# The down projection of a two-layer encoder by Strassen's scheme: seven products in place of eight, on one Trainium2 core

## The chip, the cores and the metric

The kernel runs on one core of one Trainium2 chip. The metric is the device time of one execution in microseconds (us), from the first to the last of the core's work; the time of before is the median of three runs.

## The reference

Two layers of a bidirectional encoder over 256 tokens of width 1024, float32. Each layer has a mixer (gated convolution, pooling and windowed attention) and then a gated feed-forward, which is where the change lies:

```python
    h2 = rms_norm(x, g_ffn)
    gate, up = jnp.split(h2 @ w_gu, [D_FF], axis=-1)     # D_FF = 2816
    return x + (jax.nn.silu(gate) * up) @ w_down         # w_down: 2816 x 1024
```

After the second layer one more RMSNorm gives the output.

## The kernel before, in words

Activations are held transposed: 128 rows of the model width on the partitions, the 256 tokens along the free axis. Each weight matrix is cut into 128 x 128 blocks. `plan_layer` (L36) lists the blocks of a layer in the order of use, and the host lays the stream out in that order, 16 blocks (1 MB) to a chunk. SyncE loads chunks into three buffers. A half-chunk of 8 blocks is one job of `convert` (L128): ScalarE rounds it to `hi` in the matmul's reduced format (L135), VectorE takes the rest, `lo = raw - hi` (L136). There are five `hi` and five `lo` buffers, so that a convert can start once the half-chunk five jobs earlier has been used. `advance` (L139), called when a half-chunk is first used, issues the next loads and converts.

Each product is three matmuls, for float32 accuracy: `hi` of the weights with `hi` and with `lo` of the activations, and `lo` of the weights with `hi` (`mm3`, L160 to L164). There the weights are stationary and 256 tokens move. The function `split` (L232) makes `hi` and `lo` of an activation on ScalarE and VectorE.

`ffn` (L590) works in 11 steps `q`. A step computes two gate tiles and two up tiles (32 blocks of `w_gu`, each tile the sum of 8 blocks), then the activation: sigmoid on ScalarE, times the gate, times up (L634 to L651). Its two result tiles are two of the 22 row blocks of `w_down`. The down products of step `q - 1` follow the gate and up tiles of step `q`. They are added up in four PSUM banks (`acc`), which stay occupied for the whole feed-forward; the gate and up tiles rotate through the four other banks (`newB`).

- In step 0 and 1 the input `xg` is not yet normalised: the tokens' factor `r` arrives late (`norm_stats`, `norm_rows`), and the activation applies it (L638, L641). From step 2 on the normalised tiles `hs` are used, which `make_h` (L304) computes on VectorE and ScalarE during step 0's activation.
- In layer 0 the down product has the weights stationary and 256 tokens moving (`down`, L597). The result is transposed like `x`, and `add_x` (L587) adds it bank by bank; the last two row blocks are taken bank by bank, so that the first bank ends first. `xg_tiles` (L241) and `squares` then make layer 1's inputs.
- In layer 1 the activations are stationary and 512 columns of `w_down` move (`down_nat`, L608 to L617); the result has tokens on the partitions. The four token and column quarters of `x` are transposed on TensorE during steps 4 to 7 (L671 to L676), and at the end `sums` (L718) adds a bank to each, squares it, and `rstd` and `store` write the output.

The instructions are written in the order of the source, and the framework's scheduler orders each engine's queue when the program is built: an instruction that is not ready by its estimate lets a later one pass. On the chip the queues of VectorE and ScalarE run in that order. The framework also keeps two engines from using one PSUM bank at a time.

## Time and profile before

| | us |
|---|---|
| median of 3 runs | 981.78 (981.57 to 982.46) |
| the profiled execution, its span | 980.1 |
| TensorE busy | 968.1 |
| VectorE busy | 715.7 |
| ScalarE busy | 554.0 |
| GpSimd busy | 45.7 |

The rows in the prediction name an engine (PE is TensorE's matmuls, PEld its weight loads, DVE VectorE, ACT ScalarE, POOL GpSimd), a line of the kernel, an operation with `output<-inputs`, the shape, and the count. In a list by time the first two numbers are the start and the duration; in brackets stands the idle time before it and what ended it. Matmuls are pipelined: their recorded durations overlap, and the pace is the distance between starts.

### The profile page before, as it was taken

The page shows a single profiled execution, that of the slowest core. Times are in us where ns is not written, and L with a number is a line of the kernel's source. Part 1 is how long each engine was busy: PE and PEld are TensorE (multiplying, and loading weights), DVE is VectorE, ACT ScalarE, POOL GpSimd, SP SyncE. Part 2 cuts the span into 40 slices and gives each one's busy share as a digit, 9 for nine tenths or more (in the row PEclk, how much of TensorE's full clock was granted, in tenths as well). Part 3 has the DMA queues.
Part 4 walks back from the last instruction along what each step waited for, and adds up shares of the span by engine and source line. Part 5 has one row for each costly group of instructions (what it writes and reads, how often), then busy time and mean ns, then how long its engine had stood idle before and what let it go on. Part 6 is the DMA issues. An engine that isn't in the chain of part 4 may idle for free.

```text
span 980.1 us, 19200 instructions
## 1 busy us (share of the span) xinstructions
PE 968.1 (99%) x7877; PEld 954.4 (97%) x7877; DVE 715.7 (73%) x1332; ACT 554.0 (57%) x931; POOL 45.7 (5%) x66
## 2 busy tenths in 40 slices
PE   8999999999999999999999999999999999999996
PEld 7999999999999999999999999999999999999995
DVE  7899898567668955545589898985777697555554
ACT  5866776654456544444477576765554564444443
POOL 5100000000001000000020000000000020000001
PEclk9999999999999999999999999999999999999999
DMA  8755544555554455455443745445554555545531
GB/s 279 254 193 197 189 161 163 197 180 183 189 199 171 174 189 199 173 178 205 178 172 130 248 163 188 161 143 174 192 193 173 172 194 189 200 170 204 184 129 43
DMA packets 27112, 178.12 MB, mean 182 GB/s; under 512 B 3280, under 2 KB 3808, under 8 KB 6800
## 3 DMA queue, kind: packets, MB, share of 16 engines
q1 hardware_dynamic: 24912, 169.93, 49.1%
q0 software_dynamic: 2112, 6.97, 2.5%
q8 instruction: 61, 1.00, 0.4%
q14 instruction: 27, 0.22, 0.1%
HBM read 175.80 MB, written 1.08 MB: 180 GB/s over the span
## 4 chain that ended last, share of the span: by engine, by line
PE 97%; DMA 1%; DVE 1%; SPq 0%; ACT 0%; issue 0%; DVEq 0%; ACTq 0%
PE b L162 25%; PE b L164 25%; PE b L163 25%; PE dn L164 2%; PE dn L162 2%; PE dn L163 2%; PE dn L617 2%; PE dn L616 2%; PE dn L615 2%; PE wo L162 2%; PE wo L163 2%; PE o L389 2%; PE wo L164 2%; PE pt L374 1%; DMA x<-xT 1%; PE sc L348 1%
## 5 line engine op out<-in xcount | busy, mean ns | idle before, releaser
L136 DVE TENSOR_TENSOR lo<-raw,hi 128x1024 fp32r<-128x1024 f32 (+1 forms) x321 | 390.0, 1222 | 215.2 <-ACT hi L135 214.4
L135 ACT ACTIVATE hi<-raw 128x1024 fp32r<-128x1024 f32 (+1 forms) x321 | 337.2, 1055 | 333.1 <-PE b L163 215.0
L162 PE MATMUL b<-h,hi 128*128 128x256 f32 x1344 | 379.8, 283 | 0.0
L164 PE MATMUL b<-h,lo 128*128 128x256 f32 x1344 | 378.4, 282 | 0.0
L163 PE MATMUL b<-h,hi 128*128 128x256 f32 x1344 | 378.3, 281 | 0.0
L162 PEld LDWEIGHTS b<-h,hi 128*128 128x128 f32 x1344 | 253.2, 188 | 0.2
L163 PEld LDWEIGHTS b<-h,hi 128*128 128x128 f32 x1344 | 253.1, 188 | 0.2
L164 PEld LDWEIGHTS b<-h,lo 128*128 128x128 f32 x1344 | 253.1, 188 | 0.0
L163 PE MATMUL b<-xg,hi 128*128 128x256 f32 x448 | 126.6, 283 | 1.6 <-DVE xg L250 1.6
L162 PE MATMUL b<-xg,hi 128*128 128x256 f32 x448 | 126.3, 283 | 1.1 <-DVE xg L247 0.8
L164 PE MATMUL b<-xg,lo 128*128 128x256 f32 x448 | 126.0, 282 | 0.0
L163 PEld LDWEIGHTS b<-xg,hi 128*128 128x128 f32 x448 | 84.4, 188 | 2.3 <-DVE xg L250 2.2
L162 PEld LDWEIGHTS b<-xg,hi 128*128 128x128 f32 x448 | 84.2, 188 | 1.6 <-issue 1.1
L164 PEld LDWEIGHTS b<-xg,lo 128*128 128x128 f32 x448 | 84.4, 188 | 0.0
L164 PE MATMUL dn<-fa,lo 128*128 128x256 f32 x176 | 49.5, 281 | 0.0
L163 PE MATMUL dn<-fa,hi 128*128 128x256 f32 x176 | 49.5, 281 | 0.0
L162 PE MATMUL dn<-fa,hi 128*128 128x256 f32 x176 | 49.5, 281 | 0.0
L260 POOL TENSOR_TENSOR sq<-sq,sq 128x512 f32<-128x512 f32 x12 | 16.2, 1353 | 507.3 <-DVE xg L250 315.5
L358 ACT ACTIVATE s<-s,sm 128x256 f32<-128x256 f32 x64 | 31.8, 500 | 13.0 <-DVE sm L355 13.0
L162 PE MATMUL b<-z,hi 128*128 128x256 f32 x128 | 36.4, 284 | 0.0
L164 PE MATMUL b<-z,lo 128*128 128x256 f32 x128 | 36.1, 282 | 0.0
L164 PE MATMUL b<-ao,lo 128*128 128x256 f32 x128 | 36.0, 282 | 0.0
(174 smaller groups left out, 1537.9 us busy)
## 6 DMA issues: line engine op xcount, KB each, us to landing
raw<-wst SPq DMA_DIRECT2D x158, 1024.0 KB, 4.9
bias<-stab POOLq DMA_DIRECT2D x16, 384.0 KB, 3.9
raw<-wst SPq DMA_DIRECT2D x3, 512.0 KB, 7.7
out<-xn SPq DMA_DIRECT2D x4, 256.0 KB, 2.0
x<-xT SPq DMA_DIRECT2D x3, 256.0 KB, 8.2
raw<-wst SPq DMA_DIRECT2D x2, 256.0 KB, 4.2
gf<-gfin POOLq DMA_DIRECT2D x2, 256.0 KB, 3.8
x<-xT SPq DMA_DIRECT2D x2, 128.0 KB, 4.6
```

The lines of the kernel that those rows point to most:

```text
L135: S.activation(hi[:, s], raw[:, s], AF.Copy)
L136: V.tensor_tensor(lo[:, s], raw[:, s], hi[:, s].bitcast(F32), op=ALU.subtract)
L162: PE.matmul(dst, wh, xh, start=start, stop=False, skip_group_check=skip)
L163: PE.matmul(dst, wh, xl, start=False, stop=False, skip_group_check=skip)
L164: last_mm[0] = PE.matmul(dst, wl, xh, start=False, stop=stop, skip_group_check=skip)
L260: G.tensor_tensor(st["acc"], st["acc"], sq, op=ALU.add)
L348: PE.matmul(ps[:, half(j)], qs[t][j][:, cs], kh, start=True, stop=False)
L358: S.activation(s[:, j], s[:, j], AF.Exp, bias=sm[:, 2 + j:3 + j], accum_out=sm[:, 6 + j:7 + j])
L389: PE.matmul(ps[:, half(j)], vv, pts[kt][i][:, half(j)], start=(kt == i == 0), stop=(kt == i == 1))
L615: PE.matmul(d, ah[:, cs], wh, start=(k == 0), stop=False)
L616: PE.matmul(d, ah[:, cs], wl, start=False, stop=False)
L617: PE.matmul(d, al[:, cs], wh, start=False, stop=(k == FT - 1))
```

## The change

A step's share of the down projection is a product of 2 x 2 blocks: token halves (128 tokens) by row blocks (the step's two), times row blocks by column halves (512 columns). Strassen's scheme in Winograd's form has seven block products where the plain one has eight, with sums of blocks on both sides and on the results.

- **Activations** (`forms`): the four blocks F and four sums of them, F2 (four VectorE operations on 128 columns), all split into `hi` and `lo`. They are the stationary operands; 512 weight columns move.
- **Weights** (`convert`, `take_forms`): a step's `w_down` rows are one chunk. Its jobs are A (two blocks, 1024 columns), B (one block, 512), C and D (two sums each, 1024). VectorE makes the sums in float32 from the raw chunk, right behind B's conversion.
- **Results**: seven PSUM banks hold the seven running sums M1 to M7 over all 11 steps. One bank (`G_`) is left for the gate and up tiles from step 2 on: the gate tile in its first half, the up tile in its second. So the gate, up pair of one tile is computed, then the down products of A and B of the step before, then the next pair, then C and D.
- **Activation function**: Silu on ScalarE in place of sigmoid and a multiplication on VectorE.
- **End of a layer**: the last two steps' products stand together; then VectorE combines the banks (`u2`, `u3`, `v` and the four quarters). In layer 0 the quarters, tokens on the partitions, are transposed back on TensorE (16 transposes) for `add_x`. In layer 1 the transposed `x` (and a difference of two parts of it) is put into four of the banks before the first products, so that the sums include it; the separate transposes and the additions of `x` at the end are gone.

The core of the diff:

```diff
     for q in range(NQ):
...
         else:
-            inner("gu", ns)
-        if q >= 1:
-            for k in (2 * q - 2, 2 * q - 1):
-                out.extend(("down", k, m) for m in range(8))
...
+            inner("gu", ns[0::2])
+            if q < NQ - 1:
+                down(first, q - 1)
+            inner("gu", ns[1::2])
+            if q < NQ - 1:
+                down(second, q - 1)
+    down(first + second, NQ - 2)
+    down(first + second, NQ - 1)
...
+    def convert(i):
+        c, f, _ = JOBS[i]
+        raw = raws[c]
+        n = HT * P // 2 if f == "B" else HT * P
+        if f in ("A", "B"):
+            src = raw[:, 0:n] if f == "A" else raw[:, 3 * n:4 * n]
+        elif f in ("C", "D"):
+            src = sums_[c][f == "D"]
...
+        if f == "B":
...
+            V.tensor_tensor(t.rearrange("p (a n) -> p a n", a=2),
+                            raw[:, 0:2 * n].rearrange("p (a n) -> p a n", a=2), b12, op=ALU.add)
+            V.tensor_tensor(t2[:, 0:n], t[:, 0:n], raw[:, n:2 * n], op=ALU.add)
+            V.tensor_tensor(t2[:, n:], t2[:, 0:n], raw[:, 3 * n:], op=ALU.add)
+            sums_[c] = (t, t2)
...
+        def forms(q, F):
+
+            F2 = newF()
+            V.tensor_tensor(F2[:, 0], F[:, 1], F[:, 3], op=ALU.subtract)
+            V.tensor_tensor(F2[:, 1], F2[:, 0], F[:, 0], op=ALU.subtract)
+            V.tensor_tensor(F2[:, 2], F[:, 0], F[:, 1], op=ALU.subtract)
+            V.tensor_tensor(F2[:, 3], F[:, 2], F2[:, 1], op=ALU.add)
...
+        def prod(q, i, w):
+            h, lo = fh[q]
+            a = FORM[i]
+            bank = M[i]
...
+            PE.matmul(bank, h[:, a], w[0], start=first, stop=False, skip_group_check=True)
+            PE.matmul(bank, h[:, a], w[1], start=False, stop=False, skip_group_check=True)
+            PE.matmul(bank, lo[:, a], w[0], start=False, stop=(q == NQ - 1), skip_group_check=True)
...
+        for i in (1, 3, 2, 5):
+            M[i] = newA(f"m{i}")
+        for i in (7, 6, 4):
+            M[i] = newB(f"m{i}")
...
+        down(0, 0)
+        down(0, 1)
+        G_ = newB("gu")
+        for q in range(2, NQ):
...
+                g_, u_ = G_[:, half(0)], G_[:, half(1)]
+                gu(n, hs, g_)
+                gu(FT + n, hs, u_)
+                s = t1("fs")
+                S.activation(s, g_, AF.Silu)
...
+                V.tensor_tensor(F[:, 2 * j:2 * j + 2].rearrange("p a t -> p (a t)"), s, u_, op=ALU.mult)
+                if q < NQ - 1:
+                    if j == 0:
+                        down(q - 1, 0)
+            forms(q, F)
+            if q < NQ - 1:
+                down(q - 1, 1)
...
+        down(NQ - 2, 0)
+        down(NQ - 2, 1)
...
+        prod(q, 1, w1)
+        prod(q, 6, w6)
+        u1 = c_tile("u1")
+        S.activation(u1, M[1], AF.Copy)
+        u2 = add(c_tile("u2"), u1, M[6])
+        prod(q, 7, w7)
+        u3 = add(c_tile("u3"), u2, M[7])
...
+        else:
+            prod(q, 4, w4)
+            C[1, 0] = add(c_tile("c21"), u3, M[4])
+            prod(q, 2, w2)
+            C[0, 0] = add(c_tile("c11"), u1, M[2])
+            prod(q, 5, w5)
+            v = c_tile("v")
+            sub(v, M[5], u2)
+            C[1, 1] = sub(c_tile("c22"), M[5], u3)
+            prod(q, 3, w3)
+            C[0, 1] = add(c_tile("c12"), v, M[3])
```

More of the change, by code (lines that the diff above doesn't have):

```diff
@@ L67, in plan_layer, with down @@
         out.extend(("o", k, m) for k in (6, 7) for m in (2 * j, 2 * j + 1))
+    first, second = [("A", 0), ("B", 0)], [("C", 0), ("D", 0)]
+    def down(forms, q):
+        out.extend((f, q) for f, _ in forms)
     for q in range(NQ):
@@ L160, in mm3, with take_forms @@
+    def take_forms(l, q, fs):
+        out = []
+        for f in fs:
+            i = state["use"]
+            advance(JOBS[i][2])
+            assert CHUNKS[JOBS[i][0]] == (l, q) and JOBS[i][1] == f and state["blk"] == 0
+            state["use"] += 1
+            for j in range(1 if f == "B" else 2):
+                out.append((his[i][:, j * 512:(j + 1) * 512], los[i][:, j * 512:(j + 1) * 512]))
+        return out
     def mm3(dst, key, xh, xl, start, stop, skip=False):
@@ L622, in ffn, with newF, gu @@
+        def newF():
+            return tmp.tile([P, 4, P], F32, name=nm("F"), tag="t2", bufs=8)
+        def gu(n, xs, dst):
+            ntile(l, "gu", n, xs, dst)
+        for q in range(2):
             ns = (2 * q, 2 * q + 1, FT + 2 * q, FT + 2 * q + 1)
@@ new lines, in ffn @@
+        for i in (7, 6, 4):
+            M[i] = newB(f"m{i}")
+        if last:
+            d = tmp.tile([P, 4, P], F32, name=nm("xd"), tag="t2", bufs=8)
+            V.tensor_tensor(d, x[:, 4:8, 0:P], x[:, 4:8, P:T], op=ALU.subtract)
+            for i, src in ((3, d), (2, x[:, 0:4, 0:P]), (5, x[:, 4:8, P:T]), (4, x[:, 0:4, P:T])):
+                for k in range(4):
+                    PE.matmul(M[i][:, k * P:(k + 1) * P], src[:, k], ident, start=(k == 0), stop=False,
+                              is_transpose=True, skip_group_check=True)
@@ L691, in trunk, with xn_tile @@
+        return C
+    def xn_tile(i):
+        return act.tile([P, 512], F32, name=f"xn{i}", tag="xz", bufs=8)
     gf = []
```

312 lines of the change are left out of this document (163 added, 149 removed).

## The prediction, made before the changed kernel was run

> **What bounds the kernel now.** I read the page first (busy time, then the chain that ended last), then TensorE's waits, then the timeline of one feed-forward step.
>
> ```profile
> PE 968.1 (99%) x7877; PEld 954.4 (97%) x7877; DVE 715.7 (73%) x1332; ACT 554.0 (57%) x931; POOL 45.7 (5%) x66
> ...
> PE 97%; DMA 1%; DVE 1%; SPq 0%; ACT 0%; issue 0%; DVEq 0%; ACTq 0%
> ```
>
> The chain that ended last runs on TensorE for 97% of the span. A busy PE need not be at its peak, so the waits come next (microseconds, times, longest):
>
> ```profile
> PE b L163 <- DVE xg L250: 1.6, 2, 0.9
> PE wps L180 <- DVE epst L175: 1.2, 1, 1.2
> PE b L162 <- DVE xg L247: 0.8, 1, 0.8
> PE b L162 <- ACT xg L249: 0.3, 1, 0.3
> ```
>
> These 3.9 us all belong to the first inputs; afterwards TensorE never waits. So every matmul slot taken away is a gain in full, and every wait the change brings is a loss in full. The pace of the slots, from TensorE's timeline in layer 1 (start, duration):
>
> ```profile
> 932.33 0.28 PE L162 MATMUL b<-h,hi 128*128 128x256 f32 x1
> ...
> 943.72 0.39 PE L615 MATMUL dn<-hi,fa 128*128 128x512 f32 x1
> ...
> 949.29 0.28 PE L162 MATMUL b<-h,hi 128*128 128x256 f32 x1
> ```
>
> Between the first two rows lie 96 gate and up matmuls of 256 columns (32 blocks, three each): 11.39 / 96 = 0.119 us each, whatever the 0.28 says. Then 24 down matmuls of 512 columns: 5.57 / 24 = 0.232.
>
> **The products.** The down matmuls of both layers (shortest, median and longest ns, first and last start, count):
>
> ```profile
> L162 PE MATMUL dn<-fa,hi x176: 279/281/285, 325.5 to 490.3; 128*128 128x256 f32 x176
> ...
> L615 PE MATMUL dn<-hi,fa x88: 388/392/404, 806.0 to 971.1; 128*128 128x512 f32 x88
> ```
>
> Three lines of each sort: layer 0 has 528 at 0.119 = 62.8 us, layer 1 has 264 at 0.232 = 61.2. The changed kernel has, for each of 11 row pairs, seven products of three 512-column matmuls: 21 x 0.232 = 4.87 us, 53.6 a layer. That removes 9.2 + 7.6 = 16.8 us. Sixteen x transposes of layer 1 only move (into four of the banks); sixteen new ones come at the end of layer 0, and lie in a gap priced there.
>
> **What VectorE gets.** VectorE in one step of the unchanged feed-forward (window, length, then PE, PEld, DVE, ACT):
>
> ```profile
> 345.00:362.00 17.00, 17.00 (x146) 17.00 (x145) 9.27 (x11) 7.46 (x9) 0.00 (x0) 1.00 0.53 185
> ```
>
> It is 55% busy there. Its costs when the queue is full come from its timeline at the start of layer 0's feed-forward:
>
> ```profile
> 314.39 1.23 DVE L136 TENSOR_TENSOR lo<-raw,hi 128x1024 fp32r<-128x1024 f32 x1 [0.30 <-ACT hi L135]
> ...
> 317.67 1.22 DVE L136 TENSOR_TENSOR lo<-raw,hi 128x1024 fp32r<-128x1024 f32 x1 [0.73 <-ACT hi L135]
> 318.82 0.68 DVE L638 TENSOR_TENSOR gs<-b,r 128x512 f32<-128x512 f32 x1
> ...
> 327.07 1.21 DVE L136 TENSOR_TENSOR lo<-raw,hi 128x1024 fp32r<-128x1024 f32 x1
> ...
> 330.61 0.68 DVE L640 TENSOR_TENSOR fs<-fs,gs 128x512 f32<-128x512 f32 x1
> 331.21 1.21 DVE L136 TENSOR_TENSOR lo<-raw,hi 128x1024 fp32r<-128x1024 f32 x1
> 332.34 0.68 DVE L641 TENSOR_TENSOR fs<-fs,r 128x512 f32<-128x512 f32 x1
> ...
> 334.08 0.68 DVE L647 TENSOR_TENSOR fs<-fs,b 128x512 f32<-128x512 f32 x1
> ...
> 335.81 0.75 DVE L234 TENSOR_TENSOR fa<-fs,fa 128x256 fp32r<-128x256 f32 x2
> 336.49 1.21 DVE L136 TENSOR_TENSOR lo<-raw,hi 128x1024 fp32r<-128x1024 f32 x1
> ```
>
> From start to start, 1024 columns take 1.14 us, 512 take 0.60, 256 take 0.34; 128 columns, which the trace doesn't show in this operation, I put at 0.21 by the same slope (0.15, the small steps' pace, to 0.34 as bounds: at most 0.5 us for a step's four). A steady step of the changed kernel then costs VectorE: four gate and up converts 4.56, A, C and D 3.42, B 0.60, the weight sums 2.34 (one of 1024, two of 512), two products with `u` 0.68, the four forms 0.84, their low parts 1.20: 13.6 us. TensorE's step falls from 17.1 to 11.39 + 4.87 = 16.3. So VectorE goes from 55% to 84%: it still fits, and in the steady steps I price the new work at nothing. Its cover is the five conversion buffers: a convert starts about four jobs (8 us) before its use and takes some 2.3. ScalarE's extra (half-width conversions, four-form splits) stays near 10 us of 16 and is covered too. Weight bytes and the SP queue's chunks stay the same in number; the gain loads on POOL move by a step, far from their use.
>
> **Start of the feed-forward, twice.** VectorE is not free here: above it runs from 317.67 to past 336 without a pause, with the two first steps' activations and the eight normalised tiles (`make_h`) ahead of the converts. Today nobody feels it, since the gate and up results go to fresh banks. In the changed kernel seven banks hold sums, and all further gate and up tiles share the eighth, which is `nxt[1]`: it is free only when step 1's product with `u` (L647 here, done at 334.08 + 0.68 = 334.76) has read it. The first down products start at 325.5 as now and last 4.87, so TensorE wants that bank at 330.4: already 4.4 us late with today's queue. The queue ahead of it changes by: pauses used up, -1.03 (0.30 and 0.73 above); weight sums +2.34; B is half a convert, -0.54; step 0's forms and low parts in place of two low parts and L640, +0.76; L640 of step 1 gone, -0.60; and, since the queue above shows a convert slipping into each pause between dependent operations, four or five converts ahead in place of four, 0 to +1.14. So 335.7 to 336.8: a stall of 5.3 to 6.5 us, part of it already on product 5 (weights C). The same row in layer 1, whose queue has the same order:
>
> ```profile
> 814.55 0.68 DVE L647 TENSOR_TENSOR fs<-fs,b 128x512 f32<-128x512 f32 x1
> ```
>
> ```profile
> 862.62 0.44 PE xt L673 x4
> ```
>
> Down products start at 806.0 (the first rows), the transposes of x put before them take 1.8 (four in 0.44, by the row below from the chain in order of time), so the bank is wanted at 806.0 + 4.87 + 1.8 = 812.7. It comes 0.9 to 2.1 us later than today's 815.2, at 816.1 to 817.3: a stall of 3.5 to 4.7. Both together 8.8 to 11.2; I take 11.0, as the pauses in the queue above are filled each time.
>
> **End of layer 0.** Today the last bank hands over without a gap (TensorE's, ScalarE's and VectorE's timelines there):
>
> ```profile
> 490.57 0.28 PE L164 MATMUL dn<-fa,lo 128*128 128x256 f32 x1
> 490.69 0.28 PE L162 MATMUL b<-xg,hi 128*128 128x256 f32 x1
> ```
>
> ```profile
> 485.08 1.06 ACT L135 ACTIVATE hi<-raw 128x1024 fp32r<-128x1024 f32 x1 [1.78 <-PE dn L163]
> ```
>
> ```profile
> 488.03 0.62 DVE L247 TENSOR_SCALAR xg<-x,ch 128x256 fp32r<-128x256 f32 x2
> 488.56 0.88 DVE L250 SCALAR_TENSOR_TENSOR xg<-x,ch,xg 128x256 fp32r<-128x256 f32 x2
> ```
>
> In the changed kernel the last two row pairs stand together: 9.74 us of products after the last up matmul. In that time a convert's high part (1.06) and then this VectorE queue must pass before layer 1's first matmul: convert A 1.14, product with `u` 0.34, forms 0.84, low parts 1.20, B 0.60, C and D and layer 1's first half-chunk 3.42, seven combinations 4.20, add to x 0.60, two tiles scaled 0.53, one low part 0.40, the second pair's add (its bank is reused) 0.60: 14.9 us. Two more converts of layer 1 are issued ahead of the combinations: 17.2 with them. TensorE waits 5.2 to 7.5 us, the new transposes inside that time. I take 7.0: the converts' buffers come free early when late products are passed by others.
>
> **End of layer 1.** The same queue as far as D is 7.5 us long, so product 6, second in the order, waits about 1.9 us if the order holds; if other products pass it, the combinations pile up behind the last matmul instead, 2.8. Today the last add follows the last matmul at once:
>
> ```profile
> 971.60 0.39 PE L617 MATMUL dn<-hi,fa 128*128 128x512 f32 x1
> ```
>
> ```profile
> 972.02 0.69 DVE L723 TENSOR_TENSOR xn<-xn,dn 128x512 f32<-128x512 f32 x1 [0.57 <-PE dn L617]
> ```
>
> I take 2.8; the rest of the tail stays as it is.
>
> **The clock during new pauses.** The granted clock (third number from the end) after the last matmul:
>
> ```profile
> 972.00:974.00 2.00, 0.00 (x0) 0.00 (x0) 1.67 (x4) 1.23 (x4) 0.46 (x1) 1.00 0.35 131
> 974.00:976.00 2.00, 0.00 (x0) 0.00 (x0) 1.86 (x4) 0.71 (x1) 0.80 (x1) 0.96 0.35 131
> 976.00:978.00 2.00, 0.00 (x0) 0.00 (x0) 0.00 (x0) 0.01 (x1) 0.00 (x0) 0.50 0.58 215
> ```
>
> It falls to a half about 3.8 us after TensorE stops. My stalls are broken up by products and transposes into pieces of 1 to 3.6 us, so by this row the term is 0. The Trainium skill, "TensorE: Matmul & The Clock Gate", section "Why this matters for your kernels", speaks against the change here: it asks for no idle gap over about 3 us, after which the clock goes back to half. By that rule, with the page's window of 3.4 us at half rate, I estimate 1.7 us for each such gap, up to 5 us on the sum for three places.
>
> **Sum.** -16.8 + 11.0 + 7.0 + 2.8 = +4.0 us against the profiled execution, whose span is 980.1. The runs shown have a median of 981.78, 1.7 above that span; with the same 1.7 I get 985.8.
>
> **Rivals.**
> - *The normalised tiles are not in the way (faster).* One mechanism at the start of the feed-forward: 8.25 us pass between 318.82 and 327.07, of which some 5.2 are `make_h`, whose result is first used after the down products. If the built queue runs C, D and step 1's activation ahead of it, the bank comes in time in both layers, and the 11.0 goes: 974.8. It decides once more than half of those 5.2 us moves behind. Against it: today's queue has the tiles first. For it: order within the queue follows readiness, and the new sums delay the row factors the tiles need, so that a convert may slip ahead.
> - *The one bank binds every step (slower).* After each up tile TensorE has only 2.1 us (A and B) before it needs the bank again; in that time come ScalarE's function (0.4 for 256 columns, by the slope of VectorE's rows), the product (0.42) and, if VectorE has just begun one, a convert (1.21). Nothing in the rows excludes a miss of half a microsecond. At 0.5 us in 18 steps: 985.8 + 9 = 994.8. Against it: VectorE's spare 2.7 us a step.
> - *The clock falls.* If a pause passes 3.8 us, which is nearest at the end of layer 0, and the half rate lasts as long as the fall took, 1.9 us are lost at each of one to three places: 987.7 to 991.5. The clock is known to fall here only after the last matmul; how long it stays low no row shows. The rule quoted above from the Trainium skill is this rival.
> - *The products aren't fewer.* 231 matmuls a layer stand in the code at a pace that layer 1 has today: under 1 in 100.
>
> **How the numbers follow.** Two runs of this kernel are told apart from about 0.2%, 2 us. Forecast 0.53 (its bounds, stalls of 8.8 + 5.2 + 1.9 to 11.2 + 7.5 + 2.8, give 980.9 to 986.5), first rival 0.25, one bank 0.12, clock 0.10. Of the forecast, 0.16 lies below 983.7 and counts as the same; faster is the first rival's 0.25; slower 0.59 is the rest. Most of the chance is on one side of no change, yet the first rival is too likely to leave out: the range goes down to 974.5, just under it, and up past the one-bank case to 996.
>
> **What would show it.** Right: TensorE's waits name VectorE's and ScalarE's steps of the feed-forward's second step (8 to 12 us in two places), then the x transposes and the first `b<-xg` of layer 1; 462 down matmuls at 0.232; steady steps of 16.3 us with VectorE near 84%. Wrong: no wait of over a microsecond at the two starts (first rival), waits repeated in each step on the gate bank (second), matmul starts 0.24 us apart for 256 columns after a gap (third), or a steady step much off 16.3.

## The result, and the profile after

The changed kernel takes 1025.29 us (median of 4 runs, 1023.04 to 1027.88) against 981.67 (4 runs, 981.35 to 982.46): a ratio of 1.0442 with a 95% interval of 1.0424 to 1.046. It is 43.6 us slower, far above the range of the forecast. The profiled execution's span is 1023.3 us, 43.2 more than before. The page of the changed kernel (busy time, share, instructions; then the chain that ended last):

```profile
PE 976.1 (95%) x7563; PEld 936.9 (92%) x7563; DVE 827.1 (81%) x1537; ACT 597.9 (58%) x991; POOL 45.7 (4%) x66
...
PE 83%; DVE 10%; ACT 3%; DMA 2%; issue 2%; DVEq 0%; ACTq 0%
```

TensorE has 314 instructions fewer and is nevertheless busy for longer: part of them ran under a halved clock. Of the chain, 17% lies off TensorE, where it was 3%. TensorE's waits (microseconds in all, times, longest), where before only 3.9 us at the kernel's own start stood:

```profile
PE gu L221 <- DVE F L748: 8.5, 16, 0.5
PE gu L221 <- DVE F L719: 5.7, 2, 3.2
PE m L680 <- ACT fh L292: 5.0, 2, 2.5
PE m L681 <- DVE lo L176: 4.9, 4, 3.1
PE ps L357 <- DVE rr L348: 3.8, 3, 1.8
PE xt L812 <- DVE c L769: 2.9, 1, 2.9
PE m L680 <- DVE gs L715: 2.0, 2, 1.4
```

The first row is a wait in every steady step but two. The others belong to the starts and ends of the feed-forward in both layers, but for 0.2 us of the fourth row and 0.3 of the fifth. The waits leave out what follows them (a restart, half clock), so the time is better read from starts of matmuls. TensorE's timeline: first gate matmul of the feed-forward, first gate tile of step 3, last up matmul and first matmul of the next layer; then the first two in layer 1, and the last matmul:

```profile
301.42 0.28 PE L221 MATMUL b<-xg,hi 128*128 128x256 f32 x1
...
357.96 0.39 PE L221 MATMUL gu<-h,hi 128*128 128x256 f32 x1 [0.54 <-DVE F L748]
...
493.25 0.28 PE L223 MATMUL gu<-h,lo 128*128 128x256 f32 x1
...
511.21 0.35 PE L221 MATMUL b<-xg,hi 128*128 128x256 f32 x1 [0.18 <-DVE xg L306]
...
803.92 0.28 PE L221 MATMUL b<-xg,hi 128*128 128x256 f32 x1
...
867.40 0.39 PE L221 MATMUL gu<-h,hi 128*128 128x256 f32 x1 [0.53 <-DVE F L748]
...
1012.43 0.40 PE L682 MATMUL m<-hi,fl 128*128 128x512 f32 x1
```

- Starts. To the first tile of step 3 TensorE has 288 matmuls of 256 columns and 42 of 512, and eight small ones of the norm that take 0.8 us before and after the change: 288 x 0.119 + 42 x 0.232 + 0.8 = 44.8 us, in layer 1 with the x transposes 46.6. It took 357.96 - 301.42 = 56.5 and 867.40 - 803.92 = 63.5: 11.7 and 16.9 lost.
- Steady steps last 17.25 us, where 11.39 + 4.87 = 16.26 would do; outside the starts 14 of them wait: 14 x 0.99 = 13.9.
- End of layer 0: 29 products stand behind the last up matmul (13 of the 42 had been put ahead of it), 6.7 us; from the last up matmul's successor at 493.37 it took 17.8: 11.1 lost.
- End of layer 1: the last up matmul starts at 1003.03, the last product's slot ends 9.5 us after it, 2.8 more than 29 slots; from there to the end of the span 10.6 us pass in place of 8.3: 5.2 lost together.

With the 16.8 us of removed slots, -16.8 + 28.6 + 13.9 + 11.1 + 5.2 = 42.0, against 43.2 measured; of the rest, 1.1 lies in layer 1's mixer (511.21 to 803.92, 292.7 us, where it took 291.6 before). So the question is not where the gain went (it came) but what the four losses are.

### The profile page after: what moved, and what is told of

Same layout as the page of the kernel before. It is cut to its first block, busy times and chain, and to the rows that moved or that the text cites. A ratio compares the mean times of both kernels' runs of the same rounds, so it can differ in the third digit from the quotient of the medians.

```text
span 1023.3 us, 18873 instructions
## 1 busy us (share of the span) xinstructions
PE 976.1 (95%) x7563; PEld 936.9 (92%) x7563; DVE 827.1 (81%) x1537; ACT 597.9 (58%) x991; POOL 45.7 (4%) x66
## 4 chain that ended last, share of the span: by engine, by line
PE 83%; DVE 10%; ACT 3%; DMA 2%; issue 2%; DVEq 0%; ACTq 0%
PE b L222 16%; PE b L223 16%; PE b L221 16%; PE gu L221 7%; PE gu L222 7%; PE gu L223 6%; DVE lo L176 4%; PE m L680 2%; ACT hi L175 2%; PE m L681 2%; PE m L682 2%; PE o L448 1%; DMA raw<-wst 1%; PE wo L221 1%; PE pt L433 1%
## 5 line engine op out<-in xcount | busy, mean ns | idle before, releaser
L175 ACT ACTIVATE hi<-raw 128x1024 fp32r<-128x1024 f32 (+1 forms) x321 | 327.5, 1024 | 283.1 <-PE gu L222 104.8
L221 PE MATMUL b<-h,hi 128*128 128x256 f32 x768 | 217.1, 283 | 0.0
L223 PE MATMUL b<-h,lo 128*128 128x256 f32 x768 | 216.2, 281 | 0.0
L222 PE MATMUL b<-h,hi 128*128 128x256 f32 x768 | 216.0, 281 | 0.0
L221 PE MATMUL gu<-h,hi 128*128 128x256 f32 x576 | 167.6, 291 | 14.2 <-DVE F L748 8.5
L222 PE MATMUL gu<-h,hi 128*128 128x256 f32 x576 | 163.7, 284 | 0.0
L223 PE MATMUL gu<-h,lo 128*128 128x256 f32 x576 | 163.7, 284 | 0.0
L221 PEld LDWEIGHTS b<-h,hi 128*128 128x128 f32 x768 | 144.6, 188 | 0.0
L222 PEld LDWEIGHTS b<-h,hi 128*128 128x128 f32 x768 | 144.6, 188 | 0.0
L223 PEld LDWEIGHTS b<-h,lo 128*128 128x128 f32 x768 | 144.5, 188 | 0.0
L221 PEld LDWEIGHTS gu<-h,hi 128*128 128x128 f32 x576 | 110.1, 191 | 24.7 <-DVE F L748 15.4
L222 PE MATMUL b<-xg,hi 128*128 128x256 f32 x448 | 127.5, 285 | 1.8 <-DVE xg L309 1.7
L223 PE MATMUL b<-xg,lo 128*128 128x256 f32 x448 | 126.7, 283 | 0.0
L222 PEld LDWEIGHTS gu<-h,hi 128*128 128x128 f32 x576 | 110.4, 192 | 0.1
L223 PEld LDWEIGHTS gu<-h,lo 128*128 128x128 f32 x576 | 110.1, 191 | 0.0
L222 PEld LDWEIGHTS b<-xg,hi 128*128 128x128 f32 x448 | 85.1, 190 | 2.9 <-DVE xg L309 2.7
L223 PEld LDWEIGHTS b<-xg,lo 128*128 128x128 f32 x448 | 85.1, 190 | 0.0
L681 PE MATMUL m<-lo,fh 128*128 128x512 f32 x154 | 63.6, 414 | 4.9 <-DVE lo L176 4.9
L175 ACT ACTIVATE hi<-sum 128x1024 fp32r<-128x1024 f32 x44 | 46.7, 1061 | 34.2 <-PE gu L222 29.6
```

Source lines behind the costliest of these rows:

```text
L175: S.activation(hi[:, a:b], src[:, a:b], AF.Copy)
L221: PE.matmul(dst, wh, xh, start=start, stop=False, skip_group_check=skip)
L222: PE.matmul(dst, wh, xl, start=False, stop=False, skip_group_check=skip)
L223: last_mm[0] = PE.matmul(dst, wl, xh, start=False, stop=stop, skip_group_check=skip)
L681: PE.matmul(bank, h[:, a], w[1], start=False, stop=False, skip_group_check=True)
```

## The experiments

**Four on the changed kernel itself.** First the steady step. The changed kernel's timelines around a restart, of TensorE, ScalarE and VectorE in turn:

```profile
968.44 0.28 PE L223 MATMUL gu<-h,lo 128*128 128x256 f32 x1
...
970.42 0.40 PE L682 MATMUL m<-hi,fl 128*128 128x512 f32 x1
971.35 0.39 PE L221 MATMUL gu<-h,hi 128*128 128x256 f32 x1 [0.53 <-DVE F L748]
...
968.64 1.06 ACT L175 ACTIVATE hi<-raw 128x1024 fp32r<-128x1024 f32 x1 [1.73 <-PE gu L222]
969.61 0.36 ACT L745 ACTIVATE fs<-gu 128x256 f32<-128x256 f32 x1
...
969.74 1.22 DVE L176 TENSOR_TENSOR lo<-raw,hi 128x1024 fp32r<-128x1024 f32 x1 [1.57 <-ACT hi L175]
970.88 0.41 DVE L748 TENSOR_TENSOR F<-fs,gu 128x256 f32<-128x256 f32 x1
```

The up tile's last matmul but one (L222) frees a conversion buffer, the last one (L223) makes Silu ready. One slot of 0.12 us decides: the conversion goes first on ScalarE, its low part first on VectorE, and the product with `u`, a 0.4 us step, is done at 971.29, 2.85 us after the last up matmul's start. TensorE had 2.09 us of products to bridge it. These are not those of A and B, as I had it in the prediction and in two of the expectations below: its timeline has twelve product matmuls behind a step's first tile and nine behind its second, so a product of C has moved ahead of the second tile, and the wait stands behind the nine that are left of C and D. That is one reading; that VectorE, at 80%, can't keep up is the other.

*Conversions behind Silu.*

```diff
-                S.activation(s, g_, AF.Silu)
+                sil = S.activation(s, g_, AF.Silu)
-                V.tensor_tensor(F[:, 2 * j:2 * j + 2].rearrange("p a t -> p (a t)"), s, u_, op=ALU.mult)
+                fm = V.tensor_tensor(F[:, 2 * j:2 * j + 2].rearrange("p a t -> p (a t)"), s, u_, op=ALU.mult)
...
-                        down(q - 1, 0)
+                        with tc.issue_after(sil.ins), tc.issue_after(fm.ins):
+                            down(q - 1, 0)
...
-                down(q - 1, 1)
+                with tc.issue_after(sil.ins), tc.issue_after(fm.ins):
+                    down(q - 1, 1)
```

> Nothing left out: in the steady steps the weight conversions that are issued with a half of the down products are queued behind that tile's Silu on ScalarE and behind its product with u on VectorE. Theory ANSWER: the wait for F after products A and B (0.5 us by the waits, 0.7 by the starts) goes in 16 of the 18 steps, step 16.4-16.5, total 1011 to 1015 us. Theory LOAD: the same work is only put in another order, the conversions come later and TensorE waits for them instead: 1022 to 1030 us.

1008.85 us (1008.32 to 1009.54), 16.4 below the changed kernel; 1.0278 of the kernel before (1.0262 to 1.0293). Its timelines at the same place of a step:

```profile
956.23 0.40 PE L682 MATMUL m<-hi,fl 128*128 128x512 f32 x1
956.47 0.28 PE L221 MATMUL gu<-h,hi 128*128 128x256 f32 x1
...
953.88 0.38 ACT L745 ACTIVATE fs<-gu 128x256 f32<-128x256 f32 x1 [1.89 <-PE gu L223]
954.16 1.05 ACT L175 ACTIVATE hi<-raw 128x1024 fp32r<-128x1024 f32 x1
...
954.29 0.42 DVE L748 TENSOR_TENSOR F<-fs,gu 128x256 f32<-128x256 f32 x1 [1.05 <-ACT fs L745]
```

Two neighbours have changed places, the product with `u` is done 1.15 us after the last up matmul's start (953.56) in place of 2.85, and TensorE goes from product to gate tile without a gap. (The product of C has moved back, so that twelve product matmuls now stand behind the second tile, as here, and nine behind the first; there is no gap behind those either.)

*No weight sums.* The three additions of `convert` (L183, L185, L186) are gone, C and D are converted from one constant tile:

```diff
-            V.tensor_tensor(t.rearrange("p (a n) -> p a n", a=2),
-                            raw[:, 0:2 * n].rearrange("p (a n) -> p a n", a=2), b12, op=ALU.add)
-            V.tensor_tensor(t2[:, 0:n], t[:, 0:n], raw[:, n:2 * n], op=ALU.add)
-            V.tensor_tensor(t2[:, n:], t2[:, 0:n], raw[:, 3 * n:], op=ALU.add)
-            sums_[c] = (t, t2)
+            sums_[c] = (fixed[0], fixed[0])
```

> The weight sums are left out: products with C and D take a constant tile instead (the output is not the reference's), which takes 2.34 us of VectorE out of each row pair and leaves every other instruction. Theory ANSWER: the conversion still stands ahead of Silu, the steady step stays at 16.9-17.2; the starts gain the wait for the norm chain (1.7 + 1.8 us) and some of the waits for C and D (4.9): 1014 to 1020 us. Theory LOAD: steps fall to 16.3-16.5, and with the starts 1000 to 1006 us.

1013.79 us (1012.18 to 1015.24), ratio 1.0333 (1.0315 to 1.035). One step each of the changed kernel, of the one without sums and of the one with conversions behind Silu (window, length, then PE, PEld, DVE, ACT busy):

```profile
357.96:375.21 17.25, 16.73 (x117) 15.19 (x117) 13.93 (x20) 9.40 (x13) 0.00 (x0) 1.00 0.52 186
```

```profile
362.28:379.53 17.25, 16.72 (x119) 15.20 (x118) 11.65 (x17) 9.44 (x13) 0.00 (x0) 1.00 0.52 188
```

```profile
357.41:373.75 16.34, 16.34 (x119) 15.41 (x117) 14.03 (x20) 9.53 (x12) 0.00 (x0) 1.00 0.55 199
```

This settles the steady step. VectorE relieved of 2.3 us: the step stays at 17.25. VectorE as loaded as ever, at 86% of its step, but in another order: 16.34. The load isn't the cause; the order is, of the conversions and of the two instructions that answer. The 11.5 us that the missing sums did save lie at the starts: to the first tile of step 3 these take 52.5 and 56.2 us in place of 56.5 and 63.5, and the wait for `rr` is no longer among the waits.

*Two banks.*

```diff
-        for i in (7, 6, 4):
+        for i in (7, 4):
             M[i] = newB(f"m{i}")
+        M[6] = M[4]
-        G_ = newB("gu")
+        G2 = [newB("gu"), newB("gu")]
...
+                G_ = G2[j]
```

> Products 4 and 6 add up in one bank (two of the four output quarters are no longer the reference's), so gate and up tiles of the steady steps take turns on two banks; every instruction is as before. Theory ANSWER (in each step TensorE comes back to the one gate and up bank after 2.1 us of products A and B, and ScalarE and VectorE answer 0.5 to 0.7 us too late because a weight conversion slips ahead of Silu and of the product with u): a steady step goes from 17.2 to 16.3-16.4, 14 to 16 us less in 18 steps, and a part of the wait at the two starts goes too (the bank of step 1's up tiles is no longer needed first): 1003 to 1010 us. Theory LOAD (VectorE at 80% of the step, with the sums and forms, can't keep up with the conversions): steps stay at 17.0-17.2, only the starts gain: 1018 to 1023 us.

995.13 us (993.06 to 997.33), 30.2 below the changed kernel and more than I expected of it; ratio 1.0138 (1.012 to 1.0156). The steps are 16.33 us long although the conversion still goes ahead of Silu: with a tile of 5.7 us in between, nobody waits for the answer. The surplus is at the starts. Layer 0's, in this kernel and below it in the one with conversions behind Silu (one bank):

```profile
335.78 0.36 PE L221 MATMUL gu<-h,hi 128*128 128x256 f32 x1 [0.75 <-DVE gs L715]
...
338.48 0.68 DVE L719 TENSOR_TENSOR F<-fs,b 128x512 f32<-128x512 f32 x1
```

```profile
339.63 0.55 PE L221 MATMUL gu<-h,hi 128*128 128x256 f32 x1 [2.53 <-DVE F L719]
...
338.81 0.68 DVE L719 TENSOR_TENSOR F<-fs,b 128x512 f32<-128x512 f32 x1
```

VectorE's queue delivers step 1's product with `u` at nearly the same time in both. With two banks TensorE is by then 2.7 us into its next tile. So a queue that runs late at the start costs what it does because one bank makes TensorE wait for its end.

*Normalised tiles late.*

```diff
-            forms(q, F)
-            if q == 0:
+            if q == 1:
                 hs = make_h(l, 1, st)
+            forms(q, F)
```

> Nothing left out: the eight normalised tiles (make_h) are issued behind step 1's product with u instead of behind step 0's forms. Theory TILES FIRST (the stall at both starts is the queue of VectorE with the tiles in front, as predicted): the waits for F L719 (2.5 and 3.2), gs (1.4 and 0.6) and lo of C (1.4 and 3.3) mostly go, with some of the half clock after them: 8 to 14 us less, 1011 to 1017 us; against it stands that the gate tiles then wait for the first tiles themselves. Rival (the start is late because the sums push the norm chain back, and because the conversions fill each gap): less than 4 us, 1021 to 1026 us.

1014.81 us (1011.71 to 1020.07), 10.5 below the changed kernel; ratio 1.0344 (1.0311 to 1.0376). The wait for F L719 shrinks from 5.7 us to 1.4, that for `gs` goes. As in the prediction, the tiles stood ahead of what TensorE wanted.

**Four on top of the conversions behind Silu (1008.85).** *Another bank at the start*: the shared bank is the one that step 0's gate results leave early, and products 6 and 4 of the first pair come behind step 2's first up tile.

```diff
+        G_ = newB("gu")
         for i in (7, 6, 4):
             M[i] = newB(f"m{i}")
...
-        down(0, 1)
+        w5, w7, w6, w4 = take_forms(l, 0, "CD")
+        prod(0, 5, w5)
+        prod(0, 7, w7)
-        G_ = newB("gu")
```

> On top of the kernel with the conversions behind Silu (1008.9 us), nothing left out: the shared gate and up bank takes the place of the first step's gate results, which are read early, in place of step 1's up results, and products 6 and 4 of the first row pair come behind step 2's first gate and up tile. If the starts are late because TensorE wants the bank that step 1's product with u still reads, the waits for F L719 (2.5 + 3.2 us) and gs (2.0) go, with part of the half clock behind them: 8 to 13 us less, 996 to 1001. If VectorE's queue as a whole is late there (tiles and conversions for C, whichever bank), the wait only moves on to the normalised tiles or to C: less than 4 us, 1005 to 1009.

1004.61 us (1004.2 to 1005.35), ratio 1.0234 (1.0217 to 1.0251): 4.2 less, at the edge between the two. The wait for F L719 is gone in full, and 3.3 us for the conversions of the gate tile itself have come (two waits, longest 1.9). But the total hides what the bank is worth. To the first tile of step 3 the starts take 52.3 and 57.3 us, 9.1 less than the 56.1 and 62.7 of the kernel with conversions behind Silu. Nearly 4 us of that are lost again at the ends and in layer 1's mixer, where the edit changes nothing and the waits are the same (2.52 us for the forms in both layers): there the clock now falls in other places. The 21 products behind the wait for the forms take 6.3 us in each layer, with a half clock in them, where they took 4.7 at full clock.

*Order at the ends*: the table load behind the last splits, the last pairs' conversions behind the last Silu, layer 1's first conversions behind the last combination (`lastop`; `ua` is the copy to `u1`).

```diff
-                if n == FT - 1:
-                    preload(AF.Sqrt, s[:, 0:1], scale=0.0, bias=epst)
...
+        with tc.issue_after(sil.ins), tc.issue_after(fm.ins):
             down(NQ - 2, 0)
             down(NQ - 2, 1)
             w1, w3, w2, w5, w7, w6, w4 = take_forms(l, q, "ABCD")
...
+        with tc.issue_after(ua.ins), tc.issue_after(last_split[0].ins):
+            preload(AF.Sqrt, s[:, 0:1], scale=0.0, bias=epst)
...
+            with tc.issue_after(lastop[0].ins):
+                advance(JOBS[state["use"]][2])
```

> On top of the kernel with the conversions behind Silu (1008.9 us), nothing left out: at the end of each layer the load of ScalarE's table comes behind the splits of the last row pair's forms, the last row pairs' conversions behind the last Silu and product with u, and at the end of layer 0 the next layer's conversions behind the combinations. Theory ORDER AT THE END (waits of 2.5 us for the forms in both layers, 2.9 for the combinations, and the half clock behind them): 6 to 9 us less, 1000 to 1003. Rival (the chain of forms, products, combinations, transposes and additions is that long whatever stands in between): less than 2.5 us, 1006.5 to 1009.

1015.81 us (1013.89 to 1016.54), 7.0 slower, ratio 1.0342 (1.0327 to 1.0358). Both expectations fail. The wait for the forms goes (5.0 us to 0.3) and the one for the combinations shrinks (2.9 to 1.8 and 0.5). In their place stand conversions of product weights (4.8 without the edit) and layer 1's inputs:

```profile
PE m L682 <- DVE lo L176: 6.9, 7, 3.3
...
PE b L221 <- DVE xg L307: 3.4, 2, 2.4
```

What was pushed back is needed too. Nor was it put where VectorE is free: with the conversions and sums held behind the last product with `u`, VectorE has nothing to do for 4.0 us ahead of it (482.7 to 486.6, in layer 0), and they crowd the time behind it. The run shows that this order is worse, not that no order helps.

*Pauses filled with zeros*: matmuls of a zero tile added to a sum's bank (or into the free gate and up bank) where TensorE waits.

```diff
+        def fill(bank, n, fresh=False):
+            for _ in range(n):
+                PE.matmul(bank[:, :T], warm[:, :P], warm, start=fresh, stop=fresh, skip_group_check=True)
...
+                if n == 4:
+                    fill(M[1], 20)
...
+        fill(M[1], 16)
         prod(q, 1, w1)
...
+            fill(G_, 22, True)
             for j in range(4):
                 ps = newB("xt")
```

> On top of the kernel with the conversions behind Silu (1008.9 us), nothing left out: matmuls of zeros (256 columns, 0.119 us each) are put where TensorE waits: 20 at each start of the feed-forward, 16 ahead of the last row pair's products, 22 at the end of layer 0. No wait gets shorter. Theory CLOCK (in that kernel's 2 us windows TensorE's busy time under a half clock adds up to 10.8 us, all of it behind pauses of 2 to 3 us): the clock stays up in the pauses that are filled, 4 to 8 us less, 1001 to 1005. Rival (the clock falls for another reason, or the half rate is hidden by the same waits): 1008 to 1014, the zeros costing up to some us.

1009.3 us (1008.22 to 1010.28), ratio 1.0279 (1.0264 to 1.0294). The clock did what was wanted at the end of layer 0 (granted clock third from the end of a row), here filled, then not:

```profile
498.00:500.00 2.00, 1.37 (x11) 1.05 (x11) 2.00 (x4) 0.00 (x0) 0.00 (x0) 1.00 0.85 352
500.00:502.00 2.00, 1.01 (x7) 0.60 (x6) 2.00 (x6) 1.64 (x4) 0.30 (x1) 1.00 0.00 0
```

```profile
500.00:502.00 2.00, 1.89 (x9) 1.49 (x8) 2.00 (x5) 0.00 (x0) 0.00 (x0) 0.50 0.70 295
502.00:504.00 2.00, 1.79 (x10) 1.22 (x9) 2.00 (x6) 1.90 (x4) 0.56 (x1) 0.70 0.03 8
```

Over all windows of 2 us, TensorE's busy time multiplied by the share of clock that is missing falls from 10.8 us to 6.1, and the time doesn't move. Only 1.5 us of the difference lie where zeros stand, at the end of layer 0. There, at full clock, TensorE is busy for 1.4 and 1.0 of 2 us, VectorE for 2.00 of 2.00: TensorE gets done sooner and waits longer, and layer 1 begins 0.3 us sooner, counted from step 2's first gate tile. In this place the halved clock isn't what sets the end. The other 3.2 us lie behind the two waits for `rr`, where no zeros stand and the clock stayed up in this execution without them; at the starts it fell in spite of the zeros (at 338.7 and 823.4), and in layer 1 the zeros themselves cost time. So the run doesn't say what the half clock costs at the starts.

*All three orders together*, with the starts' conversions and sums queued behind the last step of the norm's row factors (`rl`, L349):

```diff
+                with tc.issue_after(st["rl"].ins):
                     for i in range(1, 4):
                         gu(ns[i], xg, nxt[i // 2][:, half(i % 2)])
```

> Nothing left out: conversions behind Silu, the bank change at the starts, the order at the ends, and at the starts the conversions and weight sums behind the norm's row factors. If the four causes stand side by side, their gains add: 1008.9 less 8 to 13 (bank), 6 to 9 (ends) and 3 to 5 (row factors): 982 to 992 us. If they share one cause (VectorE's queue at the starts), 993 to 1000.

1005.82 us (1005.65 to 1007.17), ratio 1.0247 (1.0231 to 1.0262), above both ranges. The ends' loss eats what the starts gain: by starts of matmuls, the two starts take 11.2 us less than in the kernel with conversions behind Silu, the ends and layer 1's mixer together 9.6 more.

**The sums on GpSimd.** Three more, to shorten VectorE's queue rather than to reorder it, on top of the conversions behind Silu: the three additions issued on GpSimd, earlier than the conversion of B; the same with the normalised tiles late; and that with the low part of every second tile on GpSimd.

```diff
-            V.tensor_tensor(t2[:, 0:n], t[:, 0:n], raw[:, n:2 * n], op=ALU.add)
-            V.tensor_tensor(t2[:, n:], t2[:, 0:n], raw[:, 3 * n:], op=ALU.add)
+        G.tensor_tensor(t2[:, 0:n], t[:, 0:n], raw[:, n:2 * n], op=ALU.add)
+        G.tensor_tensor(t2[:, n:], t2[:, 0:n], raw[:, 3 * n:], op=ALU.add)
```

```diff
+            if k % 2:
+                S.activation(h, f, AF.Copy)
+                G.tensor_tensor(lo, f, h.bitcast(F32), op=ALU.subtract)
```

> On top of the kernel with the conversions behind Silu (1008.9 us), nothing left out: the weight sums go from VectorE to GpSimd, which has little to do in the feed-forward (by the row of its additions of 512 columns, 1.42 us, a pair's sums take it 5.5 to 6 us of 16.3). Theory QUEUE (starts and ends are as late as VectorE's queue there is long, and it is busy without a pause for 20 us): the sums' 2.34 us for two or three pairs go from each start and each end: 8 to 13 us less, 996 to 1001. Rival (starts and ends wait for chains, or GpSimd takes VectorE's memory time or is late for C): within 4 us of 1008.9, or slower.

> The same with the normalised tiles behind step 1's product with u, nothing left out. If the gain of that move (10.5 us by itself, on the changed kernel) adds to that of the sums on GpSimd: 986 to 992 us. If both only take the same wait away: 995 to 1001.

> The same again, nothing left out, with the low parts of every second normalised tile on GpSimd too: 4 x 0.34 us less in VectorE's queue at each start, 1 to 4 us below the kernel without it by theory QUEUE; if these tiles now come too late from GpSimd (0.8 us each), 0 to 5 us above it.

They take 1032.55 us (1030.51 to 1034.3; ratio 1.0517, 1.05 to 1.0534), 1023.82 (1021.03 to 1025.28; 1.0434, 1.0417 to 1.0451) and 1022.66 (1019.87 to 1023.91; 1.0413, 1.0395 to 1.0431). Moving the sums off VectorE costs 23.7 us, where I had expected a gain. Costliest groups of the first (count, busy us, mean ns), VectorE's and GpSimd's, and VectorE's of the kernel without the move:

```profile
L177 DVE TENSOR_TENSOR lo<-sum,hi 128x1024 fp32r<-128x1024 f32 x44 | 72.6, 1665 | 8.8 <-ACT hi L176 8.8
...
L187 POOL TENSOR_TENSOR sum<-sum,raw 128x512 f32<-128x512 f32 x22 | 44.9, 2043 | 1.7
```

```profile
L176 DVE TENSOR_TENSOR lo<-sum,hi 128x1024 fp32r<-128x1024 f32 x44 | 52.8, 1224 | 8.1 <-ACT hi L175 7.9
```

The same conversion takes 1665 ns on average in place of 1224, and GpSimd's addition of 512 columns 2043 in place of the 1417 that its additions of that size take elsewhere in the changed kernel. The work left VectorE's queue, and VectorE became slower by more than that work took: its busy time rises from 827.4 us to 868.5. The second and third kernel show the late tiles' gain once more (8.7), and nothing for the low parts (1.2, less than the runs' spread).

**Order and length at the starts.** Four last ones, on top of the conversions behind Silu: the late tiles; the late tiles without the sums; only the table load behind the splits; and late tiles, row factors first and table load together.

> Nothing left out: conversions behind Silu and behind the product with u in the steady steps, and the normalised tiles behind step 1's product with u. Each alone took 16.4 and 10.5 us off the changed kernel. If they are two separate causes (each step's answer, and VectorE's queue at the two starts), they add: 997 to 1000 us. If the late tiles' gain was partly in the steady steps: 1002 to 1008.

> The same with the weight sums left out (C and D take a constant tile, the output is not the reference's), to see how far the length of VectorE's queue at starts and ends alone reaches once the order is mended. Theory QUEUE: 2.34 us for one or two row pairs at each of two starts and two ends, with the half clock behind them, 8 to 13 us less than the kernel with the sums (984 to 991 if that is 997 to 1000). Theory ORDER ALONE (once the order is mended the sums lie beside other work): less than 4 us.

> On top of the kernel with the conversions behind Silu (1008.9 us), nothing left out, and of the end's changes only one: the load of ScalarE's table (1.28 us and 0.2 for its first use) comes behind the splits of the last row pair's forms in place of ahead of them. If that load is what the 2.5 us wait for the forms at both ends consists of for the most part: 2 to 4 us less, 1005 to 1007. If VectorE's queue comes in its place (it was busy with the conversions of C and D then): 1008 to 1010.

> Nothing left out: conversions behind Silu, normalised tiles late, the starts' conversions and weight sums behind the norm's row factors (waits of 1.7 us at both), and the table load behind the splits. If each takes its own wait away: 990 to 995 us, still above the kernel before. If the conversions put back come late in turn: 997 to 1004.

- Late tiles: 1000.07 us (997.79 to 1001.22), ratio 1.0184 (1.0169 to 1.0199). 8.8 less: the two orders, in the step and at the start, add up, nearly.
- Without the sums: 990.64 (989.41 to 991.53), ratio 1.009 (1.0075 to 1.0105). A further 9.4 us for a shorter queue, when all is in the better order, and all of it at the starts (47.1 and 50.8 us to the first tile of step 3 in place of 52.5 and 55.0). Length counts beside order. And even with this work left out, the kernel is not as fast as the one before.
- Table load alone: 1009.02 (1007.68 to 1011.05), ratio 1.028 (1.0263 to 1.0297). No change: conversions move up to where the load stood, and the forms are waited for in four pieces of 5.8 us in all, where it was two of 5.0.
- All together: 997.57 (997.1 to 999.33), ratio 1.0164 (1.0149 to 1.018). The best version in which nothing is left out: 27.7 us below the changed kernel, 16 above the one before. No run here beats that one.

## Why the prediction was wrong, step by step

- **Fewer matmuls (-16.8): right.** 462 products of 512 columns stand in the trace at 0.232 us, 0.119 for 256, and the sum of the first section closes to about 1 us with the full 16.8.
- **Steady steps priced at nothing: wrong; 13.9 us outside the starts, and with those 16.4, by the run that took it away.** This is the step that failed most clearly. The busy time was right (13.6 us forecast for VectorE, 13.93 measured), and so was its answer to whether it fits. But the cover that I named, five conversion buffers, covers conversions. The gate and up bank has no such cover: TensorE comes back to it 2.09 us after the up tile, whatever VectorE's average. My second rival had this mechanism, behind the step's other tile, with half the price (0.5 us a step; 0.99 came), and I set it at 0.12 because of VectorE's 2.7 us of spare time a step. The kernel without sums shows that argument to be void: 5.6 us to spare, and the same wait.
- **Starts (11.0): 28.6, the right place and the wrong size.** Of these, 16.0 are waits of TensorE's and 2.0 step 2's own 0.99 in each layer; the greater part of the rest are slots at a half clock. The row that I reckoned with, step 1's product with `u`, ends at 337.41 + 0.67 = 338.1 in layer 0, where I had 335.7 to 336.8. Three things are missing from my sum. The weight sums, which I had counted for VectorE's queue alone, go in front of the norm's chain too, so that TensorE waits for `rr` (1.7 and 1.8 us), before the products that my count begins with. Product C's conversion is late by itself, up to 3.1 us in layer 1. And after the wait a half clock follows: the rows below. With it the first gate and up tile of step 2 in layer 0 takes 8.3 us (338.23 to 346.53) in place of 5.7.

Starts of the first gate tile of step 2 in layer 0, TensorE's timeline of the changed kernel (0.21 us apart in place of 0.12), then two windows there:

```profile
338.23 0.55 PE L221 MATMUL gu<-h,hi 128*128 128x256 f32 x1 [2.53 <-DVE F L719]
338.58 0.41 PE L222 MATMUL gu<-h,hi 128*128 128x256 f32 x1
338.80 0.41 PE L223 MATMUL gu<-h,lo 128*128 128x256 f32 x1
```

```profile
336.00:342.00 6.00, 3.77 (x18) 3.80 (x19) 6.00 (x12) 2.11 (x3) 0.00 (x0) 0.59 0.49 175
342.00:348.00 6.00, 6.00 (x39) 5.74 (x39) 2.50 (x4) 2.39 (x3) 0.00 (x0) 0.85 0.59 205
```

  What sets the price is a product of two things that I took one at a time: a queue of VectorE that is late, and one bank that makes TensorE wait for its end. Either alone is cheaper (two banks; tiles late; no sums). My first rival, the tiles not in the way, did not come about; the runs with late tiles show that it would have been worth 8.8 to 10.5 us.
- **End of layer 0 (7.0): 11.1.** What I had priced came as I had it: TensorE waits 3.0 us for the combinations, and the transposes and the addition to x take 3.9, which makes 7.0. The two conversions of my upper bound are there, between the combinations (504.27, then `c`). Unforeseen are the 2.7 us of the wait for the last pair's forms with the restart, behind a table load and conversions on ScalarE, and 1.4 of half clock behind it:

```profile
495.75 1.28 ACT L328 ACT_TABLE_LOAD   x1
...
497.24 0.61 ACT L292 ACTIVATE fh<-F 128x512 fp32r<-128x512 f32 x1
...
497.91 0.79 PE L680 MATMUL m<-hi,fh 128*128 128x512 f32 x1 [2.52 <-ACT fh L292]
...
504.27 2.35 DVE L176 TENSOR_TENSOR lo<-raw,hi 128x1024 fp32r<-128x1024 f32 x2
506.54 1.28 DVE L769 TENSOR_TENSOR c<-u,m 128x512 f32<-128x512 f32 x2
...
507.27 3.76 PE L812 MATMUL xt<-ident,c 128*128 128x128 f32 x16 [2.88 <-DVE c L769]
```

  But neither the table load (nothing gained) nor the order that I tried (7.0 lost) is the cause of that wait in the sense that moving it helps. What would make the forms come sooner stays open; no kernel here makes the end shorter and leaves the rest.
- **End of layer 1 (2.8): 5.2.** The combinations pile up behind the last matmul, as the second case of the prediction had it, for 2.4 us; the same wait for the forms (2.5, with the restart 2.8) comes on top.
- **The clock (0): the reading was wrong, and the term isn't 0.** My third rival came about, at five places. TensorE's busy time in windows of 2 us, multiplied by the share of clock that is missing, adds up to 12.0 us in the changed kernel, so my "3.8 us after TensorE stops", read off the end of the run, does not hold for pauses. The rule of the Trainium skill that I quoted beside it (no gap over about 3 us) was the nearer one, but only two of the waits are as long as that. Not all of the 12.0 us are lost, as the zeros at the end of layer 0 show. These are: 2.6 us on step 2's first tile in layer 0 and 2.7 in layer 1, where TensorE has nothing else to wait for; 1.4 on the 21 products at the end of layer 0, which take 6.1 us from first to last start (497.91 to 503.99), where those of layer 1, at full clock, take 4.7 (1007.69 to 1012.43); and 1.5 behind the wait for `rr` in layer 1. The last is taken over from layer 0: step 2's first gate tile starts 36.8 us after the feed-forward's first matmul in the changed kernel and in the one with zeros, where the clock stays up there, and 38.3 in the one with conversions behind Silu, where it falls. By this estimate some 8 of the 43.2 us are the clock's. No run takes them away alone.
- **The range** ended at 996 because each rival was taken alone and the second at half its price. The second alone, at its measured price, would have given about 1002; that the starts cost 17.6 us more than I had, and the ends 6.5, stood for the most part in none of them.

## What to carry to other kernels

A buffer that is used again within a step asks for a prompt answer, and a share of busy time says nothing on promptness: look at what is queued, or can slip in, between the event that frees it and the instruction that answers, and put bulk work behind that answer by hand. Where a change takes spare buffers for its results, list what else lived on them, the starts and ends of the loop first, where queues are longest. And before work is moved to an idle engine, look for what it shares with the busy one.

## What the hardware did that I had not expected

*The clock falls in pauses shorter than 2 us, and not each time.* The wait for `rr` in layer 0 is 1.73 us long in the changed kernel and 1.79 in the one with conversions behind Silu. First of the one, then of the other, a stretch of 3.41 us that holds the wait, and 2 us behind it (TensorE's busy time comes first, the granted clock third from the end):

```profile
316.54:319.95 3.41, 1.68 (x14) 1.47 (x14) 2.74 (x11) 0.69 (x2) 0.00 (x0) 1.00 0.66 276
320.00:322.00 2.00, 2.00 (x19) 2.00 (x18) 2.00 (x4) 0.41 (x1) 0.00 (x0) 1.00 0.89 229
```

```profile
315.46:318.87 3.41, 1.62 (x14) 1.41 (x13) 3.20 (x11) 0.78 (x2) 0.00 (x0) 1.00 0.88 317
320.00:322.00 2.00, 2.00 (x12) 2.00 (x11) 2.00 (x4) 0.42 (x1) 0.00 (x0) 0.50 0.83 229
```

The one keeps a full clock, the other falls to a half, from 318.87 to 322.28, when the wait is already over. The stretches are chosen by the trace: within each trace of the 16 changed kernels, all changes of the granted clock but the first lie whole multiples of 3.41 us apart (337.02, 343.85, 497.45, 500.86 in the changed kernel). Cut on that grid, all 17 traces have 91 stretches at full clock after which it fell, and in 88 of them TensorE was busy for less than half of the stretch; after 4750 it stayed, and in all but five of these TensorE was busy for half or more (the 1.68 of 3.41 above is one of the five). So by these traces what counts is how much work such a stretch holds, and with it how a pause lies on the grid. This agrees with the Trainium skill, "TensorE: Matmul & The Clock Gate", section "What's actually happening", which speaks of a free-running window of about 3.4 us; that such a window need not be idle for the clock to fall, and that a pause of half its length can be enough, is this case's measurement.

*VectorE and GpSimd get in each other's way.* A conversion of 1024 columns took VectorE 1665 ns on average beside GpSimd's sums, 1224 without them, and GpSimd's additions slowed as well (2043 in place of 1417 ns). The Trainium skill, "SBUF — State Buffer", section "SBUF: two separate sides", has a port pair that VectorE with two inputs in SBUF and GpSimd hold in turn, each for a whole instruction; the rows agree in that both lose.
